# RMSNorm with Silu: the first load as two half-partition transfers, one from SyncE and one from ScalarE

## The chip, the cores and the metric

The kernel runs on one core of a Trainium2 chip. A core has five engines that matter here: VectorE (DVE), ScalarE (ACT), GpSimd (POOL), SyncE (SP, which only issues transfers and waits) and TensorE, which this kernel doesn't use. Sixteen DMA engines move data between the chip's main memory (HBM) and the core's on-chip memory (SBUF, 128 partitions). Transfers are issued by an engine's instruction queue; here SP issues the loads and ACT the stores, and in the trace they show as two DMA queues, q1 and q10.

The metric is the device time of one execution in microseconds, as the median of several runs.

## The reference

The input x has 16 x 1024 rows of 512 floats. Each row is divided by the root of its mean square (plus eps), multiplied by gamma, and passed through y * sigmoid(y), which is Silu:

```python
rms = np.sqrt(np.mean(x ** 2, axis=-1, keepdims=True) + eps)
x_norm = x / rms * gamma
return (x_norm * (1.0 / (1.0 + np.exp(-x_norm)))).astype(np.float32)
```

That is 33.55 MB in and 33.55 MB out.

## The kernel before, in words

The 16384 rows are cut into 8 groups of 2048, and in each group partition p holds 16 consecutive rows. So every partition sees 128 rows in all, and the text counts rows per partition, 0 to 127. A row over all partitions is 256 KB; 4 rows are 1 MB. On chip there is a ring of 96 rows (`xb`), worked on in place: a row is loaded, normalized, passed through Silu and stored from the same spot.

There are 12 loads, listed in `loads` as (group, row in the group, number of rows): 4, 4, 8, then four of 16, then 12 and 4 (which fill the ring), then 16, 12 and 4 into spots that must first have been stored. There are 10 stores. All loads are issued by SP from `load` (line 119), which makes SP wait for a store where the spot is still in use or where `behind` says so. The first two loads (`early = 2`) are built like the others and then moved by hand into the program's entry block, ahead of SP's drain there. The drain is the beginning of the barrier at which all engines meet before the kernel's own code starts; SP's third load and everything on the other engines stands behind this barrier.

Work goes in 32 chunks of 4 rows. For a chunk, ACT computes squares in `square`: rows 2 and 3 by an activation that also sums the row (line 164), rows 0 and 1 by one that writes the squares to PSUM (line 171), which DVE then sums (line 217). The first square of a chunk waits for the load that brings its rows (line 161). POOL adds eps and raises to the power -0.5 (lines 145 and 152). DVE multiplies each row by its factor and by gamma (line 228, four instructions). ACT applies Silu to the four rows at once (line 183). ACT runs two chunks ahead with its squares: it does square(k), then stores that are due, then Silu(k-2).

Stores are issued by ACT (line 193). Two of them are held: the store of the first 16 rows waits until the load of rows 80 to 91 has landed (line 191), and the fourth until the load of rows 112 to 123 has. So the program first only loads, then mostly stores, then loads the remainder, then stores.

Before its first square, ACT issues two small transfers: a store of a blank tile to a scratch tensor (line 197; SP waits for it once it has issued its loads) and the load of gamma (line 201, 4 partitions). DVE spreads gamma over all partitions (line 241) before its first normalization. ACT also loads its table of functions (line 204).

Of the kernel before, what the change touches and what calls it, by code (L numbers as in the profile page):

```python
# [9 lines left out]
def kernel(  # L10
# [7 lines left out]
    nc = tc.nc  # L18
    P = nc.NUM_PARTITIONS
# [4 lines left out]
    xf = x.flatten_outer_dims()  # L24
    of = out.flatten_outer_dims()
    R, D = xf.shape

    groups = [16] * 8
    slots = [0, 16, 32, 48, 64, 80, 0, 16]
    loads = [(0, 0, 4), (0, 4, 4), (0, 8, 8)]  # L30
    loads += [(g, 0, 16) for g in range(1, 5)]
    loads += [(5, 0, 12), (5, 12, 4), (6, 0, 16), (7, 0, 12), (7, 12, 4)]
    stores = [(0, 0, 16), (1, 0, 12), (1, 12, 4)]
    stores += [(g, 0, 16) for g in range(2, 7)]
    stores += [(7, 0, 8), (7, 8, 8)]
    hold = {0: (loads.index((5, 0, 12)), 12), 3: (loads.index((7, 0, 12)), 22)}
    behind = {loads.index((6, 0, 16)): 1}
    ring = 96
    early = 2
    cn = 4  # L40
    n_sq = 2

    first = [sum(groups[:g]) for g in range(len(groups))]
    assert P * sum(groups) == R, R
    assert all(s + n <= ring for s, n in zip(slots, groups))

    chunks = []
    for i, (g, r, n) in enumerate(loads):
        for c in range(r, r + n, cn):
            chunks.append((slots[g] + c, i if c == r else None))  # L50
    K = len(chunks)
    assert K * cn * P == R

    ends = [-(-(first[g] + r + n) // cn) for g, r, n in stores]

    inv_d = 1.0 / float(D)
    eps_f = float(eps)
# [4 lines left out]
    def sbuf(name, shape, dt=fp32):  # L62
        return nc.alloc_sbuf_tensor(name, shape, dt).ap()

    xb = sbuf("xb", [P, ring, D])
    gamma4 = sbuf("gamma4", [P, D])
    gamma_sb = sbuf("gamma_sb", [P, D])
    neg_half = sbuf("neg_half", [P, cn])
    ms = sbuf("ms", [P, K, cn])
    aeps = sbuf("aeps", [P, K, cn])  # L70
    rstd = sbuf("rstd", [P, K, cn])
    sq = [nc.alloc_psum_tensor(f"sq{i}", [P, n_sq, D], fp32).ap() for i in range(2)]
    junk = [nc.alloc_psum_tensor(f"junk{i}", [P, D], fp32).ap() for i in range(2)]

    ld = [nc.alloc_semaphore(f"ld{t}") for t in range(len(loads))]
# [17 lines left out]
    def need(ins, sem, value):  # L93
        return ins.wait_op(sem, value, "sem-ge")

    def dram(ap, piece):
        g, r, n = piece
        rows = ap[P * first[g] : P * (first[g] + groups[g])]
        return rows.rearrange("(p n) d -> p n d", n=groups[g])[:, r : r + n, :]

    def place(piece):
        g, r, n = piece
        return slots[g] + r, slots[g] + r + n

    def buf(piece):
        a, b = place(piece)
        return xb[:, a:b, :]

    stored_by_sync = set()

    def load(i):
        a, b = place(loads[i])
        for u, piece in enumerate(stores):
            c, d = place(piece)
            over = piece[0] < loads[i][0] and c < b and a < d
            if (over or behind.get(i) == u) and u not in stored_by_sync:
                nc.sync.wait_ge(st[u], 16)
                stored_by_sync.add(u)
        return nc.sync.dma_start(  # L119
            out=buf(loads[i]), in_=dram(xf, loads[i])  # L120
        ).then_inc(ld[i], 16)

    entry = nc.main_func.blocks[0].instructions
    here = nc.cur_bb.bb.instructions
    for t in range(early):
        ins = load(t).ins
        assert here[-1] is ins or here[-1].name == ins.name
        here.pop()
        at = next(
            i for i, other in enumerate(entry)  # L130
            if other.engine == mybir.EngineType.SP
            and isinstance(other, mybir.InstDrain)
        )
        entry.insert(at, ins)
    for t in range(early, len(loads)):
        load(t)
    nc.sync.wait_ge(s_scratch, 16)
# [4 lines left out]
    nc.gpsimd.wait_ge(s_half, 1)  # L142
    for k in range(K):
        need(
            nc.gpsimd.tensor_scalar(  # L145
                out=aeps[:, k, :], in0=ms[:, k, :], scalar1=eps_f, scalar2=None,
# [6 lines left out]
                out=rstd[:, k, :], in0=aeps[:, k, :], in1=neg_half, op=ALU.pow  # L153
# [2 lines left out]
        ).then_inc(s_rstd, 1)  # L156

    def square(k):
        at, landing = chunks[k]
        if landing is not None:  # L160
            nc.scalar.wait_ge(ld[landing], 16)  # L161
        for j in range(n_sq, cn):
            n = k * (cn - n_sq) + j - n_sq
            acc = nc.scalar.activation(  # L164
                out=junk[n % 2], in_=xb[:, at + j, :], func=AF.Square,
                scale=inv_d**0.5, accum_out=ms[:, k, j : j + 1],
            )
            if n >= 2:
                need(acc, s_acc, n - 1)
            acc.then_inc(s_acc, 1)  # L170
        square = nc.scalar.activation(  # L171
            out=sq[k % 2], in_=xb[:, at : at + n_sq, :],
            func=AF.Square, scale=inv_d**0.5,
        )
        if k >= 2:
            need(square, s_sum, k - 1)
        square.then_inc(s_sq, 1)

    def swish(k):
        at, _ = chunks[k]  # L180
        rows = xb[:, at : at + cn, :]
        need(
            nc.scalar.activation(out=rows, in_=rows, func=AF.Silu), s_norm, k + 1  # L183
        ).then_inc(s_swish, 1)
# [4 lines left out]
    def store(t):  # L189
        if t in hold:  # L190
            nc.scalar.wait_ge(ld[hold[t][0]], 16)  # L191
        need(
            nc.scalar.dma_start(out=dram(of, stores[t]), in_=buf(stores[t])),  # L193
            s_swish, ends[t],
        ).then_inc(st[t], 16)
# [9 lines left out]
    stored = 0  # L205
    for k in range(K + 3):
        if k < K:
            square(k)
        while stored < len(stores) and max(ends[stored] + 2, after(stored)) <= k:
            store(stored)  # L210
            stored += 1
        if 2 <= k < K + 2:
            swish(k - 2)
# [8 lines left out]
        ).then_inc(s_sum, 1)  # L222

    def norm(k):
        at, _ = chunks[k]
        for j in range(cn):
            row = xb[:, at + j, :]
            ins = nc.vector.scalar_tensor_tensor(  # L228
                out=row, in0=row, scalar=rstd[:, k, j : j + 1], in1=gamma_sb,
                op0=ALU.mult, op1=ALU.mult,  # L230
            )
            if j == 0:
                need(ins, s_rstd, k + 1)
        ins.then_inc(s_norm, 1)

    for k in range(K + 1):
        if k < K:
            sums(k)
        if k == 0:
            need(  # L240
                nc.vector.stream_shuffle(gamma_sb, gamma4, [0] * 32), s_gld, 16  # L241
            ).then_inc(s_gamma, 1)
        if k == 1:
            nc.vector.wait_ge(s_gamma, 1)
        if k >= 1:
            norm(k - 1)
# [39 lines left out]
```

## Time and profile before

| | us |
|---|---|
| median of 3 runs | 160.35 (160.14 to 160.46) |
| span of the profiled execution, first to last instruction | 159.0 |
| the profiled execution's own time outside its span | not given by the profile |
| ACT busy | 129.6 (82%) |
| DVE busy | 124.4 (78%) |
| POOL busy | 65.4 (41%) |
| DMA: moved 67.16 MB, mean over the span | 422 GB/s |
| loads (q1) and stores (q10), share of 16 engines' span | 49.8% and 49.2% |

Times in the profile count from the first instruction, which is SP's issue of the first load. Only computing instructions count as busy; the issue of a transfer is shown on the queue of its engine (SPq, ACTq). "DMA share" is the mean busy share of the sixteen DMA engines: a packet counts with its whole time in the stretch in which it starts, so short stretches can show more than 1. In a timeline a line gives start, duration, engine, line of the code, operation, output and input, and in brackets the idle time ahead of it with what ended it. An answer for one line of code gives smallest, median and largest duration in ns, and the first and last start in us.

### The profile page before, as it was taken

How to read it: one execution, taken by the hardware profiler on the slowest of the kernel's cores; microseconds unless marked ns; L12 is line 12 of the kernel's file. 1: busy time of each engine (PE TensorE's matmuls, PEld its weight loads, DVE VectorE, ACT ScalarE, POOL GpSimd, SP SyncE). 2: the span in 40 equal slices, each digit the busy share in tenths (PEclk: the TensorE clock that was granted, in tenths of full speed). 3: DMA queues.
4: the chain of work that ended last, by engine and by line, in shares of the span. 5: the costliest groups of instructions: out<-in, count | busy, mean ns of one | idle time of the engine just before them, and what ended most of it. 6: DMA issues, size and time to landing. Idle time of an engine off the chain costs nothing.

```text
span 159.0 us, 507 instructions
## 1 busy us (share of the span) xinstructions
DVE 124.4 (78%) x162; ACT 129.6 (82%) x193; POOL 65.4 (41%) x71
## 2 busy tenths in 40 slices
DVE  0129999999999990299999999999999999994000
ACT  0946999999999913999999999999999999947000
POOL 2035555555555550055555555555555555550000
DMA  7999999999999999989899999999999999999997
GB/s 262 441 489 396 420 486 412 396 470 453 389 422 433 433 400 433 503 367 470 363 410 396 455 408 416 443 495 420 396 462 447 412 404 478 437 396 453 387 441 301
DMA packets 3324, 67.16 MB, mean 422 GB/s; under 512 B 500, under 2 KB 500, under 8 KB 504
## 3 DMA queue, kind: packets, MB, share of 16 engines
q1 hardware_dynamic: 1728, 33.56, 49.8%
q10 hardware_dynamic: 1592, 33.57, 49.2%
q14 instruction: 4, 0.03, 0.0%
HBM read 33.56 MB, written 33.56 MB: 422 GB/s over the span
## 4 chain that ended last, share of the span: by engine, by line
ACT 65%; DMA 12%; issue 5%; DVE 4%; ACTq 2%; another core or an unknown queue 2%; SPq 0%
ACT xb L183 27%; ACT junk L164 22%; ACT sq L171 16%; DMA xb<-in_x_dram 12%; DVE xb L228 3%; ACTq L193 2%; DVE ms L217 1%; SPq L119 0%; ACTq L191 0%; ACTq L161 0%
## 5 line engine op out<-in xcount | busy, mean ns | idle before, releaser
L228 DVE SCALAR_TENSOR_TENSOR xb<-xb,rstd,gamma_sb 128x512 f32<-128x512 f32 x128 | 87.2, 744 | 0.0
L183 ACT ACTIVATE xb<-xb 128x2048 f32<-128x2048 f32 x32 | 60.9, 1902 | 10.4 <-issue 6.3
L217 DVE TENSOR_REDUCE ms<-sq 128x2 f32<-128x1024 f32 x32 | 39.1, 1223 | 17.7 <-ACT sq L171 14.5
L145 POOL TENSOR_SCALAR aeps<-ms 128x4 f32<-128x4 f32 x32 | 20.6, 644 | 71.9 <-DVE ms L217 71.9
L152 POOL TENSOR_TENSOR rstd<-aeps,neg_half 128x4 f32<-128x4 f32 x32 | 44.0, 1376 | 2.7
L164 ACT ACTIVATE junk<-xb 128x512 f32<-128x512 f32 x64 | 37.2, 582 | 3.2 <-DMA xb<-in_x_dram 3.2
L171 ACT ACTIVATE sq<-xb 128x1024 f32<-128x1024 f32 x32 | 32.2, 1005 | 0.0
L164 ACT ACTIVATION_READ_ACCUMULATOR junk<-xb 128x1 f32 x64 | 11.9, 187 | 0.0
L204 ACT ACT_TABLE_LOAD x1 | 1.3, 1283 | 3.6 <-issue 3.6
L241 DVE LOAD_MASK_SELECT gamma_sb<-gamma x1 | 0.0, 14 | 2.8 <-DMA gamma<-in_gamma_dram 2.8
L139 POOL MEMSET blank<- 128x16 f32 x1 | 0.1, 112 | 1.5 <-POOLq L60 1.5
L241 DVE STREAM_SHUFFLE gamma_sb<-gamma 128x512 f32<-128x512 f32 x1 | 0.7, 717 | 0.0
L140 POOL MEMSET gamma<- 128x512 f32 x1 | 0.5, 524 | 0.0
L267 POOL MEMSET const-float32-0.0<- 128x1 f32 x1 | 0.1, 98 | 0.2 <-issue 0.2
L267 POOL MEMSET const-uint8-127<- 128x1 uint8 x1 | 0.1, 102 | 0.0
L267 POOL MEMSET const-bfloat16-1.0<- 128x1 bf16 x1 | 0.1, 101 | 0.0
L141 POOL MEMSET neg_half<- 128x4 f32 x1 | 0.1, 101 | 0.0
L267 POOL MEMSET const-float32-1.0<- 128x1 f32 x1 | 0.1, 98 | 0.0
## 6 DMA issues: line engine op xcount, KB each, us to landing
out_dram<-xb ACTq DMA_DIRECT2D x6, 4096.0 KB, 19.2
xb<-in_x_dram SPq DMA_DIRECT2D x5, 4096.0 KB, 28.8
xb<-in_x_dram SPq DMA_DIRECT2D x2, 3072.0 KB, 37.0
xb<-in_x_dram SPq DMA_DIRECT2D x4, 1024.0 KB, 13.3
out_dram<-xb ACTq DMA_DIRECT2D x2, 2048.0 KB, 13.0
out_dram<-xb ACTq DMA_DIRECT2D x1, 3072.0 KB, 19.0
xb<-in_x_dram SPq DMA_DIRECT2D x1, 2048.0 KB, 10.3
out_dram<-xb ACTq DMA_DIRECT2D x1, 1024.0 KB, 19.8
```

The lines of the kernel that those rows point to most:

```text
L140: nc.gpsimd.memset(gamma4, 0.0).then_inc(s_zero, 1)
L145: nc.gpsimd.tensor_scalar(out=aeps[:, k, :], in0=ms[:, k, :], scalar1=eps_f, scalar2=None, op0=ALU.add,),
L152: nc.gpsimd.tensor_tensor(out=rstd[:, k, :], in0=aeps[:, k, :], in1=neg_half, op=ALU.pow),
L164: acc = nc.scalar.activation(out=junk[n % 2], in_=xb[:, at + j, :], func=AF.Square, scale=inv_d**0.5, accum_out=ms[:, k, j : j + 1],)
L171: square = nc.scalar.activation(out=sq[k % 2], in_=xb[:, at : at + n_sq, :], func=AF.Square, scale=inv_d**0.5,)
L183: nc.scalar.activation(out=rows, in_=rows, func=AF.Silu), s_norm, k + 1
L193: nc.scalar.dma_start(out=dram(of, stores[t]), in_=buf(stores[t])),
L204: nc.scalar.preload_act_table_set("silu_and_others")
L217: nc.vector.tensor_reduce(out=ms[:, k, 0:n_sq], in_=sq[k % 2], op=ALU.add, axis=mybir.AxisListType.X,),
L228: ins = nc.vector.scalar_tensor_tensor(out=row, in0=row, scalar=rstd[:, k, j : j + 1], in1=gamma_sb, op0=ALU.mult, op1=ALU.mult,)
L241: nc.vector.stream_shuffle(gamma_sb, gamma4, [0] * 32), s_gld, 16
L267: nc = _bacc.Bacc("TRN2", target_bir_lowering=False, num_devices=1)
```

## The change

The first load, rows 0 to 3 of all partitions, becomes two transfers. One takes the even partitions and is issued by SP, the other takes the odd partitions and is issued by ACT. Each is moved into the entry block ahead of the drain of the engine that issues it. Both count on the same semaphore, and ACT's first square waits for 32 instead of 16. The second load stays with SP, ahead of the barrier as before.

The same edit rewrites how pieces are named: loads and stores are now (row, number of rows) with rows from 0 to 127, the spot in the ring is the row modulo 96, and `hold` and `behind` name pieces instead of indices. The pieces, their sizes, their order, the holds and the waits between stores and loads are the same as before; in the instruction lists of the two programs only the split load and its wait differ.

```diff
+    loads = [(0, 4), (4, 4), (8, 8), (16, 16), (32, 16), (48, 16), (64, 16), (80, 12)]
+    loads += [(92, 4), (96, 16), (112, 12), (124, 4)]
+    hold = {0: ((80, 12), 12), 3: ((112, 12), 22)}
+    behind = {(96, 16): (16, 12)}
     early = 2
+    split = {(0, 4): 2}
...
+    def queue_of(i, q):
+        return nc.scalar if q else nc.sync
+
     def load(i):
...
-        return nc.sync.dma_start(
-            out=buf(loads[i]), in_=dram(xf, loads[i])
-        ).then_inc(ld[i], 16)
+        parts = split.get(loads[i], 1)
+        return [
+            queue_of(i, q).dma_start(
+                out=buf(loads[i])[q::parts], in_=dram(xf, loads[i])[q::parts]
+            ).then_inc(ld[i], 16)
+            for q in range(parts)
+        ]
...
     for t in range(early):
-        ins = load(t).ins
-        assert here[-1] is ins or here[-1].name == ins.name
-        here.pop()
-        at = next(
-            i for i, other in enumerate(entry)
-            if other.engine == mybir.EngineType.SP
-            and isinstance(other, mybir.InstDrain)
-        )
-        entry.insert(at, ins)
+        made = [one.ins for one in load(t)]
+        assert [ins.name for ins in here[-len(made) :]] == [ins.name for ins in made]
+        del here[-len(made) :]
+        for ins in made:
+            at = next(
+                i for i, other in enumerate(entry)
+                if other.engine == ins.engine and isinstance(other, mybir.InstDrain)
+            )
+            entry.insert(at, ins)
...
     def square(k):
-        at, landing = chunks[k]
-        if landing is not None:
-            nc.scalar.wait_ge(ld[landing], 16)
+        at = k * cn % ring
+        for landing in landings[k]:
+            nc.scalar.wait_ge(ld[landing], 16 * split.get(loads[landing], 1))
```

More of the change, by code (lines that the diff above doesn't have):

```diff
@@ L28 @@
     groups = [16] * 8
[L29 to L37, printed above, removed]
-    ring = 96
+    ring = 96
+    loads = [(0, 4), (4, 4), (8, 8), (16, 16), (32, 16), (48, 16), (64, 16), (80, 12)]
+    loads += [(92, 4), (96, 16), (112, 12), (124, 4)]
+    stores = [(0, 16), (16, 12), (28, 4), (32, 16), (48, 16), (64, 16), (80, 16)]
+    stores += [(96, 16), (112, 8), (120, 8)]
+    hold = {0: ((80, 12), 12), 3: ((112, 12), 22)}
+    behind = {(96, 16): (16, 12)}
     early = 2
+    split = {(0, 4): 2}
     cn = 4
@@ L43 @@
     first = [sum(groups[:g]) for g in range(len(groups))]
[L44 to L54, printed above, removed]
+    rows_each = sum(groups)
+    assert P * rows_each == R, R
+    assert ring % cn == 0
+    for pieces in (loads, stores):
+        assert [a for a, _ in pieces] == [
+            sum(n for _, n in pieces[:i]) for i in range(len(pieces))
+        ]
+        assert sum(n for _, n in pieces) == rows_each
+    K = rows_each // cn
+    hold = {t: (loads.index(piece), k) for t, (piece, k) in hold.items()}
+    behind = {loads.index(a): stores.index(b) for a, b in behind.items()}
+    landings, seen = [], 0
+    for k in range(K):
+        landings.append([])
+        while seen < len(loads) and loads[seen][0] < (k + 1) * cn:
+            landings[k].append(seen)
+            seen += 1
+    ends = [-(-(a + n) // cn) for a, n in stores]
     inv_d = 1.0 / float(D)
@@ L96, in dram @@
     def dram(ap, piece):
-        g, r, n = piece
+        a, n = piece
+        g = max(g for g in range(len(groups)) if first[g] <= a)
+        r = a - first[g]
+        assert r + n <= groups[g], piece
         rows = ap[P * first[g] : P * (first[g] + groups[g])]
         return rows.rearrange("(p n) d -> p n d", n=groups[g])[:, r : r + n, :]
-    def place(piece):
-        g, r, n = piece
-        return slots[g] + r, slots[g] + r + n
     def buf(piece):
-        a, b = place(piece)
-        return xb[:, a:b, :]
+        a, n = piece
+        at = a % ring
+        assert at + n <= ring, piece
+        return xb[:, at : at + n, :]
     stored_by_sync = set()
+    def queue_of(i, q):
+        return nc.scalar if q else nc.sync
     def load(i):
[L112 to L115, printed above, removed]
+        a, n = loads[i]
+        for u, (c, m) in enumerate(stores):
+            over = c + ring < a + n and a < c + m + ring
             if (over or behind.get(i) == u) and u not in stored_by_sync:
@@ L118, in load @@
                 stored_by_sync.add(u)
-        return nc.sync.dma_start(
-            out=buf(loads[i]), in_=dram(xf, loads[i])
-        ).then_inc(ld[i], 16)
+        parts = split.get(loads[i], 1)
[4 more added lines that the diff above has]
+            for q in range(parts)
+        ]
     entry = nc.main_func.blocks[0].instructions
@@ L179, in swish @@
     def swish(k):
-        at, _ = chunks[k]
+        at = k * cn % ring
         rows = xb[:, at : at + cn, :]
@@ L224, in norm @@
     def norm(k):
-        at, _ = chunks[k]
+        at = k * cn % ring
         for j in range(cn):
```

## The prediction

> **What bounds the kernel now.** I read the strip of 40 slices first, because it shows every engine over the whole span. What carries the argument is the row of DMA digits and the total under it.
>
> ```profile
> DVE  0129999999999990299999999999999999994000
> ACT  0946999999999913999999999999999999947000
> ...
> DMA  7999999999999999989899999999999999999997
> ...
> DMA packets 3324, 67.16 MB, mean 422 GB/s; under 512 B 500, under 2 KB 500, under 8 KB 504
> ```
>
> DVE and ACT have holes at the start, at slices 15 and 16 and at the end. The DMA engines are full from the second slice to the last but one. Busy time by stretches says the same and resolves the ramp (after the engines' columns: clock, DMA share, GB/s):
>
> ```profile
> 0.00:1.00 1.00, 0.00 (x0) 0.00 (x0) 0.19 (x4) 1.00 0.00 0
> 1.00:2.00 1.00, 0.00 (x0) 0.00 (x0) 0.11 (x2) 1.00 1.00 221
> 2.00:6.00 4.00, 0.00 (x0) 2.38 (x4) 0.50 (x3) 1.00 1.00 418
> ...
> 82.00:100.00 18.00, 17.38 (x23) 18.00 (x26) 8.46 (x9) 1.00 1.01 433
> ...
> 158.00:159.00 1.00, 0.00 (x0) 0.00 (x0) 0.00 (x0) 1.00 0.04 16
> ```
>
> Nothing moves for 1.0 us after SP begins to issue the first load. In the next microsecond the engines hold packets but move 221 GB/s. From 2.0 us on they run at 418 to 433. So the span is a silent microsecond, a half-empty one, and 67 MB at a fixed rate.
>
> The chain of waits, read third, gives ACT 65%, which seems to contradict this. Its order in time resolves it:
>
> ```profile
> 55.21 0.91 ACT sq L171
> 56.12 2.88 another core or an unknown queue
> ...
> 59.08 0.34 ACTq L193
> ```
>
> At 56.12 ACT has run out of work that it may do: its next instruction is the first store, which is held until the load of rows 80 to 91 has landed (the hold, line 191). That load lands at 59.0, and it is the DMA's date. Everything that makes ACT late by less than 2.88 us before this point is paid back here. At the other end the timeline and the line of the stores show:
>
> ```profile
> 146.82 0.34 ACTq L193 DMA_DIRECT2D out_dram<-xb  x1
> ```
>
> The same line's landings have a minimum of 12.0 us. The last store is 2.1 MB, 5.0 us at 416 GB/s, so about 7 us of older stores stand ahead of it: ACT could be late by 7 us there too. The kernel is bound by its DMA engines. The change is worth what it does to their start and to their rate, and nothing else.
>
> **The change, part by part.** The start in the trace, first the timeline, then two lines' instructions on the queues at the entry barrier, then the answers for the first loads and for the scratch store (the first transfer on ACT's queue):
>
> ```profile
> 2.49 1.09 ACTq L201 DMA_DIRECT2D gamma<-in_gamma_dram  x1
> ...
> 4.91 0.60 ACT L164 ACTIVATE junk<-xb 128x512 f32<-128x512 f32 x1
> ...
> 7.34 0.60 ACT L164 ACTIVATE junk<-xb 128x512 f32<-128x512 f32 x1 [0.18 <-DMA xb<-in_x_dram]
> ...
> 11.23 0.01 DVE L241 LOAD_MASK_SELECT gamma_sb<-gamma  x1 [2.82 <-DMA gamma<-in_gamma_dram]
> ...
> 12.23 0.60 ACT L164 ACTIVATE junk<-xb 128x512 f32<-128x512 f32 x1 [2.65 <-DMA xb<-in_x_dram]
> ```
>
> ```profile
> L267 ACTq DRAIN  x1: 8/8/8, 0.1 to 0.1; - x1
> ...
> L267 SPq DRAIN  x1: 125/125/125, 0.9 to 0.9; - x1
> ```
>
> ```profile
> L119 SPq DMA_DIRECT2D xb<-in_x_dram x12: 327/438/987, 0.0 to 80.9; - x12
> ```
>
> ```profile
> L197 ACTq DMA_DIRECT2D scratch<-blank x1: 348/348/348, 2.0 to 2.0; - x1
> ...
> DMA to landing us min/median/max: 7.9/7.9/7.9
> ```
>
> *One issue more, on ACT, ahead of its drain.* ACT reaches its drain at 0.1 us and then waits for SP, which drains at 0.9 for 0.125. An issue costs between 0.33 (the shortest on SP) and 1.09 (gamma, the longest at the start on ACT). ACT then arrives between 0.4 and 1.2, against 1.0 for SP: the barrier slips by 0 to 0.2 us. I take 0, since scratch, the nearest issue on ACT, took 0.35. Behind it on ACT stand the scratch and gamma issues, the table load, and the first square at 4.91; a slip of 0.2 moves all of them, and the 2.88 us at 56.12 cover it. SP's third load (line 119, at 1.89) would also slip, with 2 MB or 5 us of transfers still queued ahead of it. Cost: nothing.
>
> *The first load on two queues.* Bytes are the same. The second half brings one more completion write for each of 16 engines; in the rows such 4-byte and 64-byte packets take about 11 ns (52 of them are 1.8% of sixteen engines in 7 to 9 us). Cost: 0.01 us.
>
> *The silent microsecond.* The half load asks 64 partitions from each queue instead of 128. If issue and generation scale with the partitions, the first packet comes half an issue earlier: at best 0.33/2 = 0.16 us. If they don't, 0. I take 0.1, nearer the first, since both engines stand ready at 0 to 0.1.
>
> *The slow microsecond.* In quarters:
>
> ```profile
> 1.00:1.25 0.25, 0.00 (x0) 0.00 (x0) 0.00 (x0) 1.00 2.77 459
> ...
> 1.75:2.00 0.25, 0.00 (x0) 0.00 (x0) 0.11 (x2) 1.00 0.93 328
> ```
>
> 0.22 MB moved where 0.42 would: 0.20/0.42 = 0.48 us lost. A second queue could fill all of it, or none. I take none: first packets begin at 1.0 to 1.25, and the quarter from 1.75 already moves 328 GB/s and the next 393, so each engine loses only its own first packet, and it would hold just one at a time from either queue.
>
> *The rate while the halves move.* No row has a 64-partition transfer with a step of two. One bound is the 418 GB/s of 2 to 6 us: cost 0. The other is that pairs of engines get in each other's way and the whole 1.05 MB goes at half that rate: 1.05/0.418 = 2.5 us. I take 0, the nearest row being the same 8 KB packets per partition.
>
> *The wait of the first chunk* becomes one for both halves. ACT's first square starts at 4.91, right after the table load, while the load landed at 4.7 (issued at 0.0). Were the ACT half as slow as scratch, 7.9 us from issue, the square would start at 8.0, 3.1 late; two chunks of squares last from 4.91 to 9.58, so they would end at 12.7 instead of waiting 2.65 us until 12.23, and 0.5 would be left, covered at 56.12. Gamma, queued behind that half, could come 512 KB or 1.3 us later than 11.2; DVE's first four normalizations and ACT's first Silu wait for it, and again 2.88 covers it. Ring, hold and store order are the same pieces written as row numbers: no cost.
>
> Sum: -0.1 + 0.01, or -0.1 us, on the profiled execution. Its own time is not stated beside its 159.0 us span; the median of the three runs is 160.35, so 1.35 lie around the span, which I leave as they are. 160.35 - 0.1 = 160.25.
>
> [...]
>
> **The rivals.** *The ramp is filled.* For it: the engines are at half rate in the second microsecond. Against it: they are at full rate as soon as their first packets are in. Price -0.48 - 0.16 = -0.64 us at most: 159.7. It counts as faster from half of this on.
>
> *The halves collide (slower).* For it: nothing shows which engine serves which of 64 alternate partitions, and the 418 GB/s holds for a pattern in which each engine has its own eight. Against it: both halves together name the same partitions. The place is the first 1 MB; one half at half rate costs 1.25 us (161.6), both 2.5 us (162.85). It decides from an eighth of the 2.5 on, 0.32 us, for nothing later gives DMA time back.
>
> *The early start on ACT doesn't happen.* Scratch took 7.9 us for 8 KB. If a first transfer on ACT's queue is simply slow, the second load fills the engines, the first chunk is late, and the slack absorbs it: 160.35.
>
> *The engines get out of step.* The end is set by the last of sixteen. In the quarter from 1.00 the share is 2.77 for 14 packets (459 GB/s x 0.25 us / 8192 B), so a first packet takes 0.25 x 16 x 2.77/14 = 0.79 us where the rate makes 0.31. With two queues the slowest engine may lose one such excess more, 0.48 us: 160.8, and it shows wherever a later gap doesn't even it out.
>
> **How the numbers follow.** The three runs spread by 0.32 us, 0.2%, which is about what can be told from no change. Chances: forecast 0.30 (own range 160.0 to 160.5), ramp filled 0.25, ACT half late 0.13, collision 0.20, out of step 0.12. Faster is the ramp and 0.07 of the forecast's: 0.32. Same is 0.22 of the forecast and 0.12 of the late half: 0.34. Slower is the collision, most of the last case and what is left: 0.34. The range reaches from the ramp's 159.7 to 161.6, a collision of one half; beyond it lies about 0.15.
>
> **What would show it.** Right: first packets at 0.85 to 1.0 us, 410 GB/s or more in 2 to 6 us, first load landed by 5 us, the third load's issue still near 1.9, ACT still waiting between 56 and 59. The ramp rival shows as over 300 GB/s in 1 to 2 us; the collision as 200 to 350 in 2 to 6; the late half as a first square at 6 to 8 us with an unchanged rate; the last as DMA work after the rest has ended. The forecast is wrong if the load of rows 80 to 91 lands more than 0.3 us off 59.0.

## The result and the profile after

The changed kernel takes 160.68 us (median of 9, 160.62 to 161.05) against 160.31 (median of 9, 160.14 to 160.67): a ratio of 1.0024, 95% interval 1.0014 to 1.0034, so it is 0.37 us slower. The forecast was 0.1 us faster. The time lies inside the range, but it moved the other way.

The same views as before, now of the changed kernel. The strip and the total:

```profile
DMA  6999999999999999999899999999999999999997
...
DMA packets 3341, 67.16 MB, mean 422 GB/s; under 512 B 517, under 2 KB 517, under 8 KB 521
```

Busy time by stretches, with clock, DMA share and GB/s at the end of a line:

```profile
0.00:1.00 1.00, 0.00 (x0) 0.00 (x0) 0.19 (x4) 1.00 0.00 0
1.00:2.00 1.00, 0.00 (x0) 0.00 (x0) 0.00 (x0) 1.00 0.79 188
2.00:6.00 4.00, 0.00 (x0) 2.06 (x4) 0.61 (x3) 1.00 0.96 395
...
82.00:100.00 18.00, 17.38 (x23) 18.00 (x26) 8.32 (x10) 1.00 0.98 421
...
158.00:159.00 1.00, 0.00 (x0) 0.00 (x0) 0.00 (x0) 1.00 0.20 82
```

Of the strip's 40 digits the first has fallen by one and one in the middle has risen. The DMA engines are as full as before, on the same bytes, and still work in the last microsecond (82 GB/s, before 16). The loss is in the ramp: counted by bytes from the packets' own times, the changed kernel is 0.27 us behind the kernel before at 3 us and 0.28 us at 59. In quarters:

```profile
1.00:1.25 0.25, 0.00 (x0) 0.00 (x0) 0.00 (x0) 1.00 0.00 0
1.25:1.50 0.25, 0.00 (x0) 0.00 (x0) 0.00 (x0) 1.00 1.46 328
```

Before, fourteen first packets began between 1.00 and 1.25 us; now none does. The first packet begins at 1.34 us instead of 1.01. The reason stands ahead of it, on the queues that issue. First the start of the kernel before, then of the changed one (start, duration, queue, line, transfer):

```profile
0.00 0.36 SPq L119 DMA_DIRECT2D xb<-in_x_dram  x1
```

```profile
0.00 0.56 SPq L131 DMA_DIRECT2D xb<-in_x_dram  x1
0.12 0.57 ACTq L131 DMA_DIRECT2D xb<-in_x_dram  x1
```

SP needs 0.56 us to issue half of the load where it needed 0.36 for the whole. That is 0.20 of the 0.33 us; the first packet also comes 0.78 us after the issue has ended instead of 0.65. The runs below repeat both figures (0.77 to 0.80 us where a half or a quarter comes first, 0.62 to 0.67 where a whole load does), and none says why. The drains at the entry barrier of the changed kernel, in ns, then us:

```profile
L281 ACTq DRAIN  x1: 510/510/510, 0.7 to 0.7; - x1
L281 SPq DRAIN  x1: 125/125/125, 1.2 to 1.2; - x1
```

SP, not ACT, is again the last at the barrier. It drains at 1.2 instead of 0.9, since its second issue, a whole one behind the half, also took 0.57 us (before 0.42). SP's third load is issued at 2.23 instead of 1.89. Further on, the chain of waits in order of time:

```profile
55.68 0.91 ACT sq L185
56.59 2.79 another core or an unknown queue
...
59.47 0.34 ACTq L207
```

ACT still waits for the load of rows 80 to 91, for 2.79 us instead of 2.88. That load has landed at 59.39 instead of 59.00: the lateness of the first packet, handed on by DMA engines that have no time left over in between (a share of 1.01 from 6 to 56 us in both kernels). The span is 159.3 instead of 159.0, the last packet ends 0.2 us later, and around the span 1.3 us are left as before.

### The profile page after: what moved, and what is told of

The parts are those of the page before. It is cut to its first block, busy times and chain, and to the rows that moved or that the text cites. A ratio compares the mean times of both kernels' runs of the same rounds, so it can differ in the third digit from the quotient of the medians.

```text
span 159.3 us, 508 instructions
## 1 busy us (share of the span) xinstructions
DVE 124.4 (78%) x162; ACT 129.6 (81%) x193; POOL 65.4 (41%) x71
## 4 chain that ended last, share of the span: by engine, by line
ACT 65%; DMA 12%; issue 5%; DVE 4%; ACTq 2%; another core or an unknown queue 2%; SPq 0%
ACT xb L197 27%; ACT junk L178 22%; ACT sq L185 16%; DMA xb<-in_x_dram 12%; DVE xb L242 3%; ACTq L207 2%; DVE ms L231 1%; SPq L131 0%; ACTq L205 0%; ACTq L175 0%
```

## The experiments

Three theories could explain the late start: two engines issuing at once (1), the shape of the transfer (2), or the number of transfers issued ahead of the barrier (3). The ratios compare with runs of the kernel before on the same chip, whose medians were 160.25 to 160.35 us.

| run | first issue, us | first packets, us | median, us | ratio, 95% interval |
|---|---|---|---|---|
| before, in the first comparison | 0.36 | 1.01 | 160.31 | 1 |
| changed kernel | 0.56 | 1.34 | 160.68 | 1.0024, 1.0014 to 1.0034 |
| both halves on SP | 0.55 | 1.33 | 161.40 | 1.0071, 1.0052 to 1.0091 |
| second load whole on ACT | 0.36 | 0.99 | 160.66 | 1.0024, 1.0013 to 1.0035 |
| one load ahead of the barrier | 0.37 | 1.00 | 161.41 | 1.0076, 1.0057 to 1.0095 |
| ACT's half behind the barrier | 0.55 | 1.32 | 163.83 | 1.0197, 1.0174 to 1.0221 |
| halves by rows | 0.36 | 0.99 | 160.60 | 1.0023, 1.0005 to 1.0040 |
| halves by blocks of partitions | 0.54 | 1.34 | 163.08 | 1.0172, 1.0154 to 1.0191 |
| second load split instead | 0.37 | 1.00 | 160.39 | 1.0001, 0.9987 to 1.0014 |
| quarters | 0.54 | 1.32 | 161.37 | 1.0062, 1.0032 to 1.0092 |
| whole load, late by one issue | 0.42, begun at 0.42 | 1.50 | 160.88 | 1.0036, 1.0021 to 1.0050 |
| first two loads as one | 0.37 | 1.00 | 160.44 | 1.0002, 0.9986 to 1.0019 |

The first two columns are from the profiled execution of each run, the first packets from the times of its DMA packets of 4 KB and more.

### Both halves from SP

```diff
     def queue_of(i, q):
-        return nc.scalar if q else nc.sync
+        return nc.sync
```

> Both halves of the first load are issued by SP, one after the other; ACT issues nothing ahead of the barrier. Three theories of the late start that the changed kernel shows (SP's first issue 0.56 us instead of 0.36, first packets at 1.34 us instead of 1.01). Theory 1, two issuers: SP and ACT issuing at the same time slow each other. It expects a first issue of 0.36 us, first packets near 1.0 us and 160.3 us. Theory 2, the shape: a transfer over 64 partitions with a step of two is slow to issue, whoever issues it. It expects 0.56 us, 1.34 us and 160.65 us. Theory 3, the number: the first packets wait for all transfers issued ahead of the barrier, 0.33 us for each. It expects three issues, so 1.34 us and 160.65 us even with short issues.

The first lines of its timeline and its quarters:

```profile
0.00 0.55 SPq L131 DMA_DIRECT2D xb<-in_x_dram  x1
```

```profile
1.00:1.25 0.25, 0.00 (x0) 0.00 (x0) 0.00 (x0) 1.00 0.00 0
1.25:1.50 0.25, 0.00 (x0) 0.00 (x0) 0.00 (x0) 1.00 1.59 328
```

With ACT silent the first issue is as slow and the first packet as late. Theory 1 is out as the cause of the late packet. The time is 0.7 us longer than theories 2 and 3 allow. SP issues three transfers here, so its third load leaves at 2.86 us instead of 1.89. The profiled execution (160.71 us, the quickest of six) shows a brief gap only at 4 us, so what the others lost is not shown.

### The second load whole on ACT

```diff
-    split = {(0, 4): 2}
+    split = {}
...
-        return nc.scalar if q else nc.sync
+        return nc.scalar if i == 1 else nc.sync
```

> No halves: SP issues the first load whole and ACT the second load whole, 128 partitions each, both ahead of the barrier. Theory 1, two issuers, expects SP's first issue at 0.56 us, first packets near 1.34 us and 160.65 us. Theory 2, the shape, expects 0.36 us, 1.0 us and 160.3 us. Theory 3, the number, counts two transfers as in the kernel before: 1.0 us and 160.3 us.

```profile
0.00 0.36 SPq L131 DMA_DIRECT2D xb<-in_x_dram  x1
0.13 0.39 ACTq L131 DMA_DIRECT2D xb<-in_x_dram  x1
```

Two engines issue 0.13 us apart, each at the price of a whole transfer, and the first packets come at 0.99. That agrees with theory 2 against theory 1. Theories 2 and 3 missed the time by 0.4 us. The start is right, but ACT's queue now carries 1 MB ahead of gamma, and DVE waits for gamma until 18.29 us instead of 11.23:

```profile
18.29 0.01 DVE L255 LOAD_MASK_SELECT gamma_sb<-gamma  x1 [8.40 <-DMA gamma<-in_gamma_dram]
```

ACT then has no wait left at 56 us, and the first stores leave when ACT gets to them. This could be a second way to lose time, and the changed kernel doesn't take it: its gamma lands at 11.53. That it accounts for the 0.4 us isn't shown: in the profiled execution, one of the quicker ones at 160.47 us, the first store leaves at 59.14 us, 0.06 later than before, and only half of the loss is there.

### One load ahead of the barrier

```diff
-    early = 2
+    early = 1
```

> The kernel before with only its first load ahead of the barrier; the second follows right behind the barrier on SP. Theories 1 and 2 expect the first packets where they were, at 1.0 us, and 160.3 us, as 1 MB covers the engines until the second load's packets come. Theory 3, the number, expects the first packets at 0.7 us and 160.0 us.

First packets come at 1.0 us, so theory 3 is out. The time went up by 1.2 us (0.9 to 1.5) against everybody's expectation. Busy time of its stretch from 4 to 7 us:

```profile
4.00:7.00 3.00, 0.00 (x0) 2.62 (x6) 0.00 (x0) 1.00 0.95 305
```

The kernel before moves 441 GB/s there. The second load was issued at 1.43 us, and its packets follow on the first load's from 4.0 us, but eight of them, begun between 4.0 and 4.5, take 0.66 to 1.55 us where 0.31 is usual. The kernel's very first packets were as slow (0.43 to 1.17 us); the kernel before shows no such packets when its second load begins. From 4 to 5 us the DMA engines are also idle for 0.14 us. So the second load ahead of the barrier is worth 1.2 us here; why its packets start slowly from behind the barrier was not tested.

### ACT's half behind the barrier

```diff
-        made = [one.ins for one in load(t)]
...
+        made = [ins for ins in made if ins.engine == mybir.EngineType.SP]
```

Only SP's instructions are moved into the entry block.

> SP issues the even half and the second load ahead of the barrier as in the changed kernel, ACT issues the odd half only behind the barrier, at about 1.9 us. Theory 1, two issuers, expects SP's first issue at 0.36 us, first packets at 1.0 us and 160.3 us; the first chunk is late by 1 to 3 us, which the wait at 56 us takes up. Theory 2, the shape, expects 0.56 us, 1.34 us and 160.65 us. Theory 3, the number, expects two transfers, 1.0 us and 160.3 us.

The first issue and packet go with theory 2. The time, 3.2 us up by the ratio, was expected by none, and shows that ACT's wait at 56 us covers only so much. The late half was issued at 2.23 and its packets began at 6.15. The timeline of ACT, its longest waits, and the DMA engines when the stores should begin:

```profile
10.91 0.60 ACT L179 ACTIVATE junk<-xb 128x512 f32<-128x512 f32 x1 [5.07 <-DMA xb<-in_x_dram]
```

```profile
DVE gamma_sb L256 <- DMA gamma<-in_gamma_dram: 7.4, 1, 7.4
```

```profile
61.00:64.00 3.00, 2.86 (x4) 3.00 (x4) 1.12 (x2) 1.00 0.42 180
```

The first square starts 6.0 us late, gamma lands at 21.8, ACT issues the first store only at 62.5 instead of 59.1, and with no store to move the DMA engines stand idle for some 2.9 us between 60 and 64.

### Halves by rows

```diff
-    loads = [(0, 4), (4, 4), (8, 8), (16, 16), (32, 16), (48, 16), (64, 16), (80, 12)]
+    loads = [(0, 2), (2, 2), (4, 4), (8, 8), (16, 16), (32, 16), (48, 16), (64, 16), (80, 12)]
-    early = 2
-    split = {(0, 4): 2}
+    early = 3
+    split = {}
...
-        return nc.scalar if q else nc.sync
+        return nc.scalar if i == 1 else nc.sync
```

> The first four rows in two transfers again, one from SP and one from ACT, both ahead of the barrier, but cut by rows: rows 0 and 1 of all 128 partitions from SP, rows 2 and 3 of all 128 from ACT. Theory 2, the shape (fewer than 128 partitions, or a step, makes the issue slow), expects SP's first issue back at 0.36 us, first packets at 1.0 us and 160.3 us. The rival, that two queues at the start cost by themselves (the run with the whole second load on ACT was 0.4 us slower with first packets at 1.0 us), expects the same start and 160.6 us.

The first four rows come in two transfers from two engines, yet whole in partitions: the issue is back at 0.36 us, the packets at 0.99, the third load at 1.89. That is theory 2 for the start. The time fits the rival. Counted by bytes from the packets' own times, it is 0.15 us behind the kernel before at 5 us, as ACT's 4 KB packets begun between 3.5 and 4.3 us take up to 0.49 us where 0.16 is usual, and 0.15 more from 60 to 61 us, where the DMA engines are busy for only 0.84 of the time. What causes either was not tested. So curing the issue did not make the two queues pay.

### Halves by blocks of partitions

```diff
-                out=buf(loads[i])[q::parts], in_=dram(xf, loads[i])[q::parts]
+                out=buf(loads[i])[q * P // parts : (q + 1) * P // parts],
+                in_=dram(xf, loads[i])[q * P // parts : (q + 1) * P // parts],
```

> As the changed kernel, but partitions 0 to 63 from SP and 64 to 127 from ACT, so no step. If the step is what is slow, SP's first issue takes 0.36 us, first packets come at 1.0 us, and the time is 160.3 us. If the number of partitions is, 0.56 us, 1.34 us and 160.65 us. If halves of neighbouring partitions also get in each other's way, the rate from 2 to 6 us falls below 350 GB/s and the time is over 161 us.

```profile
2.00:6.00 4.00, 0.00 (x0) 1.28 (x1) 0.61 (x3) 1.00 1.00 236
```

The issue is slow without a step too (0.54 us, first packets 1.34), so the step isn't the cause. And here is a loss like the one that the prediction feared from a collision: 236 GB/s instead of 395, and 2.4 us on the median against the changed kernel, close to the 2.5 us that the rival's bound gave. Even and odd partitions don't have it (395 GB/s). The halves come mostly one after the other (SP's packets from 1.34 to 4.2 us, ACT's from 3.2 to 6.5), at 238 GB/s from 2 to 4 us and 234 from 4 to 6, with the DMA engines holding packets meanwhile (shares of 0.93 and 1.08). What slows them was not shown.

### The second load split instead

```diff
-    split = {(0, 4): 2}
+    split = {(4, 4): 2}
```

> The same split into even and odd partitions, from SP and ACT, made on the second load instead of the first; the first is whole, from SP. If the price of the changed kernel is the late first packet alone, SP's first issue is 0.36 us, the slow issues lie beside the first load's 2.5 us of transfers, first packets come at 1.0 us and the time is 160.3 us. If the slow issues cost through the later barrier, or wherever they stand, it is 160.65 us.

```profile
0.00 0.37 SPq L131 DMA_DIRECT2D xb<-in_x_dram  x1
```

```profile
1.00:1.25 0.25, 0.00 (x0) 0.00 (x0) 0.00 (x0) 1.00 1.71 328
```

The same two slow issues (0.53 and 0.57 us), the same two queues, a barrier as late (third load at 2.27 us), and no price: 1.0001, 0.9987 to 1.0014. So two queues at the start are not dear by themselves, nor is the late barrier. What costs in the changed kernel is that the half transfer is the very first.

### Quarters

```diff
-    split = {(0, 4): 2}
+    split = {(0, 4): 4}
...
-        return nc.scalar if q else nc.sync
+        return nc.scalar if q % 2 else nc.sync
```

> The first load in four transfers of every fourth partition, two from SP and two from ACT. If an issue is slower the fewer partitions it names (0.36 us for 128, 0.56 for 64, 1.09 for the gamma load with 4), SP's first issue takes 0.6 to 0.8 us, first packets come at 1.4 to 1.7 us, and the time is 160.8 to 161.0 us. If 0.56 us is the price of any transfer that isn't whole, first packets come at 1.34 us.

The first issue is 0.54 us and the first packet comes at 1.32: no slower than for halves. So "the fewer the partitions, the slower" is wrong. The time is 1.0 us up, with the third load issued at 2.85 as in the run with both halves on SP, and with an idle third of a microsecond at 60 us; why there was not tested.

### A whole first load, one issue late

```diff
+    def ahead():
+        return nc.sync.dma_start(out=probe, in_=xf[0:P, 0:16]).then_inc(s_probe, 16)
+
-    for t in range(early):
-        ins = load(t).ins
+    for t in range(-1, early):
+        ins = (load(t) if t >= 0 else ahead()).ins
```

> The kernel before, with one tiny load over all 128 partitions (64 B each, into a tile that nothing uses) issued by SP ahead of the first load. No half transfer, and nothing on ACT: only the first load is late, by one whole issue of about 0.41 us. If a late first packet costs its lateness to the end, the first load's packets start at 1.4 us and the time is 160.7 us. If a start that is 0.4 us late is made up later, 160.3 us.

```profile
0.00 0.36 SPq L128 DMA_DIRECT2D probe<-in_x_dram  x1
...
0.42 0.42 SPq L121 DMA_DIRECT2D xb<-in_x_dram  x1
```

The first load's packets start at 1.50 us, 0.49 late, and the time is 0.36% or 0.6 us up (0.3 to 0.8). No half transfer and no issue on ACT is in it. So a late first packet costs time at the end, within the interval as much as it was late. In the profiled execution, one of the quicker ones at 160.61 us, it is 0.47 to 0.49 us behind by bytes from 6 to 80 us, and 0.3 us from 100 us on.

### The first two loads as one

```diff
-    loads = [(0, 0, 4), (0, 4, 4), (0, 8, 8)]
+    loads = [(0, 0, 8), (0, 8, 8)]
...
-    early = 2
+    early = 1
```

> The first two loads of the kernel before joined into one of eight rows, ahead of the barrier: one whole issue instead of two. First packets at 1.0 us as before; the barrier opens 0.4 us earlier, which nothing waits for; packets of 16 KB instead of 8 KB save some 0.05 us on each DMA engine; ACT's first square waits until about 7 us, and the wait at 56 us takes that up. All theories expect 160.2 to 160.3 us. If ACT's late start is not taken up, 161 us or more.

No difference that can be told: 1.0002. Here one issue with 2 MB behind it does what two with 1 MB each do. It is no way to a kernel faster than the one before.

### What an issue costs by its shape

Two runs put seven unused loads on SP behind its last load, each issued when the one ahead had landed, so that nothing else stood in the way. Each is a single execution. The second makes the kernel longer (173.9 us), as SP's own loads come to the end.

```diff
     nc.sync.wait_ge(s_scratch, 16)
+    o, i = rows_of(64, 2)
+    nc.sync.dma_start(out=o, in_=i).then_inc(s_probe[3], 16)
+    nc.sync.wait_ge(s_probe[3], 16)
```

> The kernel before, with seven tiny loads (64 B per partition, into a tile that nothing uses) on SP behind its last load, each issued only when the one ahead has landed: 128 partitions, 96, 64, 64 with a step of two, 32, 16, and 4 with a step of 32. It measures the issue alone. Theory 2 with the price on every transfer that isn't whole expects 0.33 to 0.36 us for 128 and about 0.55 us for all the others down to 16; if the gamma load's 1.07 us is also a matter of shape, the last form takes about 1.0 us, and if that was waiting behind another queue's issues, 0.55 us.

> The issue alone again, now with the first load's own element of 8 KB per partition and its own source: seven loads into a tile that nothing uses, on SP behind its last load, each issued when the one ahead has landed: 128 partitions twice (the first stands right behind three other issues), 64, 64 with a step of two, 32, 32 with a step of four, 96. In the run with 64 B per partition 96, 32 and 16 partitions took 0.32 to 0.34 us and 64 took 0.49 to 0.54; in the run with quarters 32 with a step of four took 0.54 to 0.58. If the step makes it slow, both stepped forms take about 0.55 us and 32 without a step 0.33. If 64 partitions are slow in any form, 64 takes 0.55 us with and without a step. If it is the time of the issue and not the form, the two 128 differ as much as the forms do.

With 8 KB per partition, in the order 128 (right behind other issues), 128, 64, 64 with a step of two, 32, 32 with a step of four, 96; durations in ns:

```profile
L145 SPq DMA_DIRECT2D probe<-in_x_dram x1: 442/442/442, 81.3 to 81.3; - x1
...
L148 SPq DMA_DIRECT2D probe<-in_x_dram x1: 328/328/328, 108.9 to 108.9; - x1
...
L151 SPq DMA_DIRECT2D probe<-in_x_dram x1: 544/544/544, 124.9 to 124.9; - x1
...
L154 SPq DMA_DIRECT2D probe<-in_x_dram x1: 479/479/479, 137.0 to 137.0; - x1
...
L157 SPq DMA_DIRECT2D probe<-in_x_dram x1: 346/346/346, 148.0 to 148.0; - x1
...
L160 SPq DMA_DIRECT2D probe<-in_x_dram x1: 474/474/474, 156.9 to 156.9; - x1
...
L163 SPq DMA_DIRECT2D probe<-in_x_dram x1: 328/328/328, 164.0 to 164.0; - x1
```

With 64 B per partition: 128, again right behind other issues, took 0.49, 64 took 0.54, 64 with a step of two 0.49, 96 took 0.34, 32 took 0.33, 16 took 0.32, and 4 with a step of 32 took 0.61:

```profile
L163 SPq DMA_DIRECT2D probe<-in_x_dram x1: 609/609/609, 146.8 to 146.8; - x1
```

Standing behind other issues is worth 0.11 us (the two 128 with 8 KB), less than the 0.13 to 0.22 us between the slow forms and the quick ones. So 64 partitions are slow in every form tried (0.48 to 0.58 us), whether 64 B or 8 KB are behind each; 96, 32 and 16 neighbouring partitions cost what 128 do (0.32 to 0.35 us against 0.33); 32 with a step of four is slow again (0.47). The expectation that every transfer short of 128 pays is refuted. What the rule is stays open: neither the number of partitions nor a step alone sorts these rows.

## Why the prediction was wrong

**What bounds the kernel: right.** The bound was put at the DMA engines, with only their start and their rate able to move the time. The run with a whole but late first load agrees: 0.49 us of start gave 0.6 us (0.3 to 0.8) at the end.

**The silent microsecond: the step that failed.** It set the first packet 0 to 0.16 us earlier and took 0.1. It came 0.33 us later, since the half's issue took 0.56 us instead of 0.36 and its first packet then came 0.78 us after the issue instead of 0.65. The error is in the bound: half an issue was taken as the best case and an unchanged issue as the worst, with nothing on the side of a loss. The row that denies this stood in the prediction. Gamma, with 4 partitions, took 1.09 us on ACT where scratch, with 128, took 0.35. It was read as an upper price for ACT's arrival at the barrier, and not as a sign that an issue over fewer partitions can be dearer. Part of that 1.09 may have been waiting, as a load of the same four partitions alone took 0.61, but as an upper bound it would have been enough: 1.09 less 0.36 is 0.7 us of possible delay. Why an issue over 64 partitions is slow stays open. The prediction's own sign of being wrong came in: the load of rows 80 to 91 landed 0.39 us later.

**The sum.** With +0.33 for this term in place of -0.1 and the other terms as they were, it gives +0.34 us; measured 0.37 us (ratio 1.0014 to 1.0034, so 0.2 to 0.5).

**One issue more on ACT, ahead of its drain: no cost, as said, but with another cause.** The barrier slipped by 0.34 us, beyond the 0 to 0.2 forecast, and it was SP's own issues that made it slip. The second load split instead has a slip of 0.38 and no price.

**The slow microsecond: right.** The second queue fills nothing. DMA packets by queue of the changed kernel, from 2.9 to 4.2 us:

```profile
q10 hardware_dynamic: 61, 0.49, 90.4%
q1 hardware_dynamic: 23, 0.06, 11.1%
```

ACT's half, issued at 0.12 us, has no packet before 2.92, when all but a few of the 64 packets of SP's half have begun. The two hardly run side by side; they follow each other, and the first still needs its own start.

**The rate: right.** 395 GB/s from 2 to 6 us, with the late start in it, isn't a collision: from 4 to 6 us it is 418, before 427. The collision rival named a loss that exists at about its price (2.4 us against 2.5), but with halves of neighbouring partitions.

**The slack: right here, overstated in general.** First square at 5.23, wait at 56 still 2.79 us. But with a half whose first packet is late by 3.2 us more (6.15 against 2.92), the run with ACT's half behind the barrier lost 3.2 us. The prediction had let gamma's lateness of 1.3 us through; where ACT's queue holds more, gamma lands at 18 to 22 us and ACT has no wait left at 56 us to take it up.

**The slower rivals.** Both named another mechanism than the one that happened. Their chance of 0.34 for slower came out for a reason that wasn't among them. That 160.68 lies near the 160.8 of the engines out of step is luck: the loss is there by 3 us, and the work left in the last microsecond (82 GB/s), which was to be that rival's sign, is the same in the run with a late whole load from SP alone.

**Two issuers.** With a whole load on each engine, issuing from two engines brought SP's third load forward (1.59 us instead of 1.89). With halves it did the reverse (2.23 us): two issues of 0.56 and 0.57 us stand in place of one of 0.36.

## What to carry to other kernels

In a kernel bound by its DMA engines, price what the first transfer's issue takes before its first packet, since that lateness is still there at the end (0.33 us gave 0.37, 0.49 gave 0.6), while the same slow issue one transfer later was free (1.0001). Don't scale an issue with its partitions (64 took 0.48 to 0.58 us here, 32 and 16 neighbouring ones 0.32 to 0.35): look for rows of the same shape in the trace, and where there are none, let the bound reach to the dearest odd-shaped issue in it. And ask of any second queue what stands behind the new transfer on it, as gamma did here.

## What the runs showed that was not expected

- An issue over 64 partitions takes 0.48 to 0.58 us on SP and ACT, one over 128, 96, 32 or 16 neighbouring ones 0.32 to 0.39 where nothing holds it up; a whole one right behind a half took 0.57.
- The second queue's packets start late: a half issued at 0.12 us began at 2.92, one issued at 2.23 at 6.15, and a scratch store issued at 2.04 (kernel before) at 5.50. In the changed kernel and in the run with quarters the first pieces are taken nearly one after the other; with a whole load on each queue the packets alternate from 2.7 us on.
- A drain right behind a 64-partition issue on ACT takes 0.38 to 0.51 us (on SP 0.40); behind whole issues it took 0.12 to 0.15.
- Moving the second load from ahead of the barrier to behind it costs 1.2 us, though 1 MB is under way at the time: its first packets are slow (0.66 to 1.55 us instead of 0.31).
